# Activations or weights as the moving operand: the SwiGLU and output products of a four-layer encoder

## The chip, the core and the metric

The kernel runs on one core of a Trainium2 chip. The metric is device time in microseconds (us) of one execution, the median of several runs. TensorE (PE) multiplies: a load of weights (LDWEIGHTS, row PEld in the profile) puts a stationary operand of up to 128x128 into the array, and a MATMUL streams the columns of a moving operand past it and adds the result into a bank of PSUM, 128 partitions by 512 float32. VectorE (DVE), ScalarE (ACT) and GpSimd (POOL) work element by element, and SyncE (SP) and others start the transfers (DMA) from the main memory. Engines wait for each other by semaphores.

## The reference

Four layers, each with a token mixer and a SwiGLU, both behind an RMS norm and added to the residual. 256 tokens, 1024 features, 2816 hidden units, all float32.

```
for i in range(4):
    x = x + mixer[i % 3](rmsnorm(x, g_mix[i]))     # short convolution, attention, Hyena, short convolution
    h = rmsnorm(x, g_ffn[i])
    g, u = split(h @ w13[i])                       # 1024 -> 2 x 2816
    x = x + (silu(g) * u) @ w2[i]                  # 2816 -> 1024
```

Mixer A is `w_out((B * conv3(C * h)))`, mixer B an attention in a window of the 4 x 64 grid of tokens, mixer C a Hyena operator (two long convolutions as products with Fourier matrices; its filters depend on no input x and are made beside the SwiGLU stages of layers 0 and 1). Each mixer ends in an output projection of 1024 x 1024.

## The kernel before

*Layout.* The residual X lies by feature: 8 tiles of 128 features by 256 tokens (line 81). Every product of the trunk is made in three parts to keep float32's accuracy at the rate of float32r: with hi = the value rounded to float32r and lo the rest, hi*hi + hi*lo + lo*hi, which is `mm3` (lines 113 to 118). A weight piece of 128 x 1024 is loaded by SP (L104), rounded by ACT (L105) and its low part made by DVE or, for a share, by POOL (L108, recorded as L74). There are five buffers for loaded pieces and six for their parts, so pieces run some way ahead.

*Products.* In `mm3` the weight is stationary and the activation moves: 128 x 128 of the weight against 128 features x 256 tokens. Output tiles are by feature. Only mixer B's input product (`rows`, lines 493 to 502) has it the other way round, with 256 columns of the weight moving.

*Norm.* `Norm.add` (L134) multiplies a residual tile by the gain and splits it into the two parts xs (ACT L137, DVE L138) and squares it (ACT L155; DVE adds). The factor 1/rms belongs to a token, so it is applied to what comes out: `stats` (L158) turns the sum of squares by two PE transposes, `expand` (L173) turns 1/rms back and spreads it over all partitions as R.

*SwiGLU* (`ffn`, L259). w13: 11 pairs of hidden column tiles; for each pair four weight pieces (two of g, two of u), eight matmul triples each, into the banks pg and pu. A stage later `gated` multiplies both by R (tg, tu), takes Silu and the product (hh), and splits it into the two parts hid. w2: eight output tiles po of 22 triples; as each is done, `residual` (L184) adds it to X and prepares that tile of the next norm.

*Output projections* (`OutProj`, L202). The rows of w_out are taken as the mixer delivers its tiles: six of eight (AHEAD) go into all eight output tiles at once, four banks; for the last two, `finish` goes output tile by output tile, each followed by its residual and norm tile. The first products after a norm go through the k tiles in the order in which these come (`in_group`).

*Order.* The program is recorded in the order of the code, with stages of the pipelines delayed by slots of a weight piece each (`Pipeline`), and a scheduler then sets the order of each engine by what is ready. `fill(j)` lets the Hyena filters go on by a step at given places of the SwiGLU. Each engine works through its own list in that fixed order; a PSUM bank or a part buffer is taken again when its last reader is done.

In names of tiles, digits tell layers and numbers: xsf2 is the norm of layer 2's SwiGLU (xsf; f0 to f3), xsm3 that of layer 3's mixer (m0 to m3), hiw and low the parts of a SwiGLU weight, accco the output projection of mixer C.

Of the kernel before, what the change touches and what calls it, by code (L numbers as in the profile page):

```python
# [9 lines left out]
F32 = mybir.dt.float32  # L10
# [8 lines left out]
P = 128  # L19
# [10 lines left out]
# columns of the per-partition vector table  # L30
# [21 lines left out]
def encoder(ctx: ExitStack, tc: tile.TileContext, A: dict, out: bass.AP):  # L52
# [23 lines left out]
    def v2(a):  # L76
        """[P, 512] as two halves."""
        return a.rearrange("p (i t) -> p i t", i=2)

# [1 line left out]
    X = const.tile([P, KT, T], F32, name="X")  # L81
# [38 lines left out]
    def split(hl, src):  # L120
        """hl[:, 0] + hl[:, 1] = src, both float32r; the parts lie along axis 1."""
        ac.copy(out=hl[:, 0], in_=src)
        tt(hl[:, 1], src, hl[:, 0].bitcast(F32), ALU.subtract)

    class Norm:
        """The pre-norm of the next sub-layer: x times the gain as the operand of
        its products, and 1 / rms by token for what comes out of them."""

        def __init__(self, gcol, name):
            self.g, self.name, self.xs, self.late = gcol, name, {}, []  # L130
            self.ss = tp.tile([P, T], F32, tag="ss", name=f"ss{name}", bufs=2)
            self.R, self.some = None, False

        def add(self, m, square=True):  # L134
            xm, g = X[:, m, :], vec[:, self.g + m : self.g + m + 1]
            xs = xsp.tile([P, 2, T], F32R, tag="xs", name=f"xs{self.name}_{m}")
            ac.activation(xs[:, 0], xm, AF.Copy, scale=g)  # L137
            ve.scalar_tensor_tensor(  # L138
                out=xs[:, 1], in0=xm, scalar=g, in1=xs[:, 0].bitcast(F32),
# [3 lines left out]
            if square:  # L143
                self.square(m)
            else:
                self.late.append(m)

        def square(self, m):
            xm = X[:, m, :]
            if not self.some:  # L150
                self.some = True
                ac.activation(self.ss, xm, AF.Square)
            else:
                sq = t1(f"sq{self.name}_{m}")
                ac.activation(sq, xm, AF.Square)  # L155
                tt(self.ss, self.ss, sq, ALU.add)

        def stats(self):  # L158
            """1 / rms, the tokens on the partitions."""
            n = self.name  # L160
            for m in self.late:
                self.square(m)
            ps = self.ps = bank(f"psn{n}")
            ms = tp.tile([P, 2], F32, tag="ms", name=f"ms{n}", bufs=2)
            for i in range(2):
                pe.transpose(ps[:, i * P : (i + 1) * P], self.ss[:, i * P : (i + 1) * P], ident)
            ve.tensor_reduce(out=ms, in_=ps[:, :T].rearrange("p (i f) -> p i f", i=2), axis=AX.X, op=ALU.add)
            ve.tensor_scalar(out=ms, in0=ms, scalar1=1.0 / D, scalar2=EPS,
                             op0=ALU.mult, op1=ALU.add)
            rt = self.rt = tp.tile([P, 2], F32, tag="rt", name=f"rt{n}", bufs=2)  # L170
# [13 lines left out]
    def residual(m, ps, norm):  # L184
        tt(X[:, m, :], X[:, m, :], ps, ALU.add)
        if norm is not None:
            norm.add(m)
# [743 lines left out]
```

## Time and profile before

| what | us |
|---|---|
| three runs | 1257.48, 1259.48, 1259.76 |
| median | 1259.48 |
| span of the profiled execution | 1256.2 |
| mean granted TensorE clock of it | 0.990 of 2.4 GHz |
| matmuls and weight loads recorded | 10,034 each |
| PE busy in the span | 1219.3 (97%) |
| VectorE, ScalarE, GpSimd | 913.4, 634.6, 269.8 |
| moved by DMA | 228.90 MB, 182 GB/s in the mean |

The profile is of one execution; its span goes from its first instruction to its last, and what the device adds around it is in the runs' times alone (1.3 to 3.6 us here). A matmul is recorded with a modelled end, so that successive ones overlap: the distance from start to start tells the pace, not the duration. The granted clock is the share of 2.4 GHz that the chip gives TensorE; it is 1.00 in most stretches and 0.50 in a few.

### The profile page before, as it was taken

To read this page: it belongs to the slowest core of one execution; us is meant where nothing else is said; L and a number is where in the kernel's file an instruction comes from. 1 tells how busy PE (TensorE), PEld (TensorE's weight loads), DVE (VectorE), ACT (ScalarE), POOL (GpSimd) and SP (SyncE) were. 2 spreads that over 40 slices of the span, in tenths; PEclk is the share of its full clock that TensorE was granted. 3 is DMA by queue.
4 is the path that set the end of the run, shared out by engine and by line. 5 is a ranking of instruction groups with operands and counts; after the bars stand their busy time and mean duration, and the time that the engine had idled before them with its cause. 6 is when DMAs were issued, how large, how long until landed. Compare 5 with 4: busy or idle time off the path is not lost.

```text
span 1256.2 us, 24460 instructions
## 1 busy us (share of the span) xinstructions
PE 1219.3 (97%) x10034; PEld 1211.2 (96%) x10034; DVE 913.4 (73%) x1156; ACT 634.6 (51%) x931; POOL 269.8 (21%) x228
## 2 busy tenths in 40 slices
PE   7999999999999999999988979999999999999998
PEld 7999999999998999999988879999999999999998
DVE  7766877887776688878869997766655676766642
ACT  6545554555667554545544345444444455444431
POOL 0111122333454023213347773000000000000000
PEclk9999999999999999999998989999999999999999
DMA  9556556666666365666754324655566565655571
GB/s 307 184 175 229 185 173 193 201 191 222 209 178 194 118 218 186 192 187 191 232 179 135 121 98 155 199 184 185 173 185 197 176 188 163 199 185 185 170 203 46
DMA packets 68505, 228.90 MB, mean 182 GB/s; under 512 B 9831, under 2 KB 11241, under 8 KB 68265
## 3 DMA queue, kind: packets, MB, share of 16 engines
q1 hardware_dynamic: 61408, 211.68, 53.8%
q0 software_dynamic: 4656, 9.73, 2.6%
q10 hardware_dynamic: 2328, 5.93, 1.4%
q8 instruction: 78, 1.28, 0.4%
q14 instruction: 35, 0.28, 0.1%
HBM read 220.99 MB, written 6.29 MB: 181 GB/s over the span
## 4 chain that ended last, share of the span: by engine, by line
PE 84%; DVE 8%; issue 2%; ACT 2%; DMA 2%; POOL 2%; SPq 0%; ACTq 0%; DVEq 0%; POOLq 0%
PE pu L116 7%; PE pg L116 7%; PE pg L118 7%; PE pu L117 7%; PE pg L117 7%; PE pu L118 7%; PE po L116 7%; PE po L118 7%; PE po L117 7%; DVE a L74 1%; PE ai1a L117 1%; PE ai1a L116 1%; PE ai1a L118 1%; PE accao L116 1%; PE accao L117 1%
## 5 line engine op out<-in xcount | busy, mean ns | idle before, releaser
L105 ACT CAST hiw<-stw 128x1024 fp32r<-128x1024 f32 (+1 forms) x276 | 280.5, 1024 | 314.3 <-PE pg L117 85.3
L74 DVE TENSOR_TENSOR low<-stw,hiw 128x1024 fp32r<-128x1024 f32 (+1 forms) x254 | 306.2, 1212 | 155.1 <-ACT hiw L105 153.8
L116 PE MATMUL pu<-xsf,hiw 128*128 128x256 f32 x704 | 199.9, 284 | 0.0
L116 PE MATMUL pg<-xsf,hiw 128*128 128x256 f32 x704 | 199.3, 283 | 0.0
L118 PE MATMUL pg<-xsf,low 128*128 128x256 f32 x704 | 199.2, 283 | 0.0
L117 PE MATMUL pu<-xsf,hiw 128*128 128x256 f32 x704 | 199.2, 283 | 0.0
L117 PE MATMUL pg<-xsf,hiw 128*128 128x256 f32 x704 | 199.2, 283 | 0.0
L118 PE MATMUL pu<-xsf,low 128*128 128x256 f32 x704 | 199.2, 283 | 0.0
L116 PE MATMUL po<-hid,hiw 128*128 128x256 f32 x704 | 197.5, 281 | 0.0
L117 PE MATMUL po<-hid,hiw 128*128 128x256 f32 x704 | 197.5, 281 | 0.0
L118 PE MATMUL po<-hid,low 128*128 128x256 f32 x704 | 197.5, 281 | 0.0
L116 PEld LDWEIGHTS pg<-xsf,hiw 128*128 128x128 f32 x704 | 134.6, 191 | 0.3 <-issue 0.3
L116 PEld LDWEIGHTS pu<-xsf,hiw 128*128 128x128 f32 x704 | 134.5, 191 | 0.3 <-ACT hiw L105 0.3
L118 PEld LDWEIGHTS pg<-xsf,low 128*128 128x128 f32 x704 | 134.6, 191 | 0.0
L117 PEld LDWEIGHTS pg<-xsf,hiw 128*128 128x128 f32 x704 | 134.6, 191 | 0.0
L117 PEld LDWEIGHTS pu<-xsf,hiw 128*128 128x128 f32 x704 | 134.6, 191 | 0.0
L118 PEld LDWEIGHTS pu<-xsf,low 128*128 128x128 f32 x704 | 134.5, 191 | 0.0
L116 PEld LDWEIGHTS po<-hid,hiw 128*128 128x128 f32 x704 | 132.4, 188 | 0.0
L117 PEld LDWEIGHTS po<-hid,hiw 128*128 128x128 f32 x704 | 132.4, 188 | 0.0
L118 PEld LDWEIGHTS po<-hid,low 128*128 128x128 f32 x704 | 132.4, 188 | 0.0
L74 POOL TENSOR_TENSOR low<-stw,hiw 128x1024 fp32r<-128x1024 f32 (+1 forms) x22 | 53.6, 2434 | 158.8 <-ACT hiw L105 150.8
L105 ACT CAST hiai<-stai 128x1024 fp32r<-128x1024 f32 (+1 forms) x49 | 49.0, 1014 | 49.0 <-issue 13.3
(246 smaller groups left out, 2922.3 us busy)
## 6 DMA issues: line engine op xcount, KB each, us to landing
stw<-in_f_w SPq DMA_DIRECT2D x208, 512.0 KB, 3.6
stw<-in_f_w SPq DMA_DIRECT2D x64, 448.0 KB, 3.4
stai<-in_a_w_in SPq DMA_DIRECT2D x45, 512.0 KB, 3.7
stbi<-in_b_w_qkv SPq DMA_DIRECT2D x24, 512.0 KB, 4.3
stci<-in_c_w_in SPq DMA_DIRECT2D x24, 512.0 KB, 4.0
stao<-in_a_w_out SPq DMA_DIRECT2D x16, 512.0 KB, 4.3
hf<-ht POOLq DMA_DIRECT2D x16, 256.0 KB, 2.7
stbo<-in_b_w_out SPq DMA_DIRECT2D x8, 512.0 KB, 4.0
```

Of the source, the lines that this page charges most:

```text
L74: (eng or ve).tensor_tensor(out=out_, in0=a, in1=b, op=op)
L105: ac.copy(out=hi[:, c], in_=st[:, c])
L116: pe.matmul(ps, hi[:, ws], xh, start=first, stop=False, **kw)
L117: pe.matmul(ps, hi[:, ws], xl, start=False, stop=False, **kw)
L118: pe.matmul(ps, lo[:, ws], xh, start=False, stop=last, **kw)
```

## The change

The residual X now lies by token (two tiles of 128 tokens by 1024 features), and in SwiGLU and in the output projections the activation is the stationary operand, 128 x 128 of it, while 512 columns of the weight stream past.

- w13: a pair of hidden tiles has two banks, one for each half of the tokens, with 256 columns of g beside 256 of u. Silu and the product then work by token, where 1/rms is one value per partition: ACT's scale and DVE's scalar take the place of R. The gated tile hh is by token and must be by hidden unit to be stationary in w2: `turned` turns it by four PE transposes into a bank, from which it is split.
- w2 and the output projections: one class `OutProj` for both. All output is in four banks (two halves of the features by two of the tokens). The rows of the weight are taken as they come, up to the last four (w2, HELD) or three (AHEAD is 5); for those it goes bank by bank, and each bank is added to X when it is done.
- Norm: the next sub-layer still needs x by feature. `turn` turns a bank's worth of X (four transposes, one norm has four such turns), ACT and DVE make the xs tiles from PSUM, and ACT squares X by token with the sum as an extra output. The last of the four turns, `flush`, comes within the next sub-layer's first products, after half of their k tiles.
- The input comes once by feature, for the first norm, and once by token, 1 MB, in mixer A. The output leaves by token in four transfers of 256 KB.
- The weights w13 and w2 lie in main memory in the order in which they are now loaded.

The input products of mixers A, B and C are as before. Comments are left out of the code.

```diff
-AHEAD = 6  # rows of an output projection that are taken as they come
+TURN_LAG = 1
+AHEAD = 5
+HELD = 4
...
-    X = const.tile([P, KT, T], F32, name="X")
+    X = const.tile([P, 2, D], F32, name="X")
...
+    def matmul3(ps, xh, xl, hi, lo, first, last):
+        pe.matmul(ps, xh, hi, start=first, stop=False, skip_group_check=True)
+        pe.matmul(ps, xl, hi, start=False, stop=False, skip_group_check=True)
+        pe.matmul(ps, xh, lo, start=False, stop=last, skip_group_check=True)
...
+        def turn(self, c, h):
+            if h == 0:
+                self.banks[c] = [bank(f"pt{self.name}{c}{i}") for i in range(2)]
+            for i in range(4):
+                pe.transpose(self.banks[c][i % 2][:, i // 2 * T + h * P : i // 2 * T + (h + 1) * P],
+                             X[:, h, c * 512 + i * P : c * 512 + (i + 1) * P], ident)
+            if h:
+                for i in range(4):
+                    self.part(4 * c + i, self.banks[c][i % 2][:, i // 2 * T : (i // 2 + 1) * T])
+                for h in range(2):
+                    self.square(c, h)
...
+        def square(self, c, h):
+            sq = t2(f"sq{self.name}{c}{h}")
+            ac.activation(sq, X[:, h, c * 512 : (c + 1) * 512], AF.Square, accum_out=self.ss[:, h, c : c + 1])
...
-        for n, (k, xs) in enumerate(norm.xs.items()):
+        for k in range(KT):
+            if k == KT // 2:
+                norm.flush()
+            xs = norm.xs[k]
...
-        def mul(self, m, k, mid):
-            mm3(self.acc[m // 2][:, (m % 2) * T : (m % 2 + 1) * T], self.parts[k],
-                slice(m * P, (m + 1) * P), mid[:, 0], mid[:, 1],
-                k == 0 and m % 2 == 0, k == KT - 1, skip=True)
+        def mul(self, c, h, k, mid):
+            hi, lo = self.parts[k]
+            t, cs = slice(h * P, (h + 1) * P), slice(c * 512, (c + 1) * 512)
+            matmul3(self.acc[c, h], mid[:, 0, t], mid[:, 1, t], hi[:, cs], lo[:, cs], k == 0, k == self.n - 1)
...
+            for c, h in self.acc:
+                for k in range(self.ahead, self.n):
+                    self.mul(c, h, k, mids[k])
+                xm = X[:, h, c * 512 : (c + 1) * 512]
+                tt(xm, xm, self.acc[c, h], ALU.add)
+                if norm is None:
+                    sy.dma_start(out=out[h][:, c * 512 : (c + 1) * 512], in_=xm)
+                elif before:
+                    norm.turn(*before)
+                before = c, h
...
-                tg, tu = t2(f"tg{layer}_{j}"), t2(f"tu{layer}_{j}")
-                tt(v2(tg), v2(pg), norm.R2(), ALU.mult)
-                sg = t2(f"sg{layer}_{j}")
-                ac.activation(sg, tg, AF.Silu)
-                tt(v2(tu), v2(pu), norm.R2(), ALU.mult)
                 hh = t2(f"hh{layer}_{j}")
-                tt(hh, sg, tu, ALU.mult)
-                h = hp.tile([P, 2, 2, T], F32R, tag="hid", name=f"hid{layer}_{j}")
-                split(h.rearrange("p i s t -> p s i t"), v2(hh))
-                hid.append(h)
-                fill(j)
+                for h in range(2):
+                    r = norm.rt[:, h : h + 1]
+                    sg = t1(f"sg{layer}_{j}{h}")
+                    ac.activation(sg, ps[h][:, :T], AF.Silu, scale=r)
+                    ve.scalar_tensor_tensor(out=hh[:, h * T : (h + 1) * T], in0=ps[h][:, T:], scalar=r, in1=sg,
+                                            op0=ALU.mult, op1=ALU.mult)
+                line.add(line.now + TURN_LAG, turned, j, hh)
...
+            def turned(j, hh):
+                pt = bank(f"pth{layer}_{j}")
+                for i in range(2):
+                    for h in range(2):
+                        pe.transpose(pt[:, i * T + h * P : i * T + (h + 1) * P],
+                                     hh[:, h * T + i * P : h * T + (i + 1) * P], ident)
+                h = hp.tile([P, 2, 2, T], F32R, tag="hid", name=f"hid{layer}_{j}")
+                split(h.rearrange("p i s t -> p s i t"), v2(pt))
+                hid.extend([h[:, 0], h[:, 1]])
+                fill(j)
...
+            for k in range(FT - HELD):
+                if k == 16:
+                    share[0] = 0
+                op.step(k, hid[k] if k < len(hid) else None)
                 line.tick()
...
+                if k % 2 and k < 16:
+                    fill(NP_ + k // 2)
...
+                if ia == 0 and m == 3:
+                    sy.dma_start(out=X, in_=A["xt"])
```

How the instructions move is shown at two places. On PE, at the end of layer 2's SwiGLU, before: po2_7 is the last output tile, ai1a0 the first product of mixer A in layer 3, whose norm is xsm3.

```order
L116 MATMUL po2_7_11691<-hid2_10_11046,hiw2_2_7_15_11750 128x256
L117 MATMUL po2_7_11691<-hid2_10_11046,hiw2_2_7_15_11750 128x256
L118 MATMUL po2_7_11691<-hid2_10_11046,low2_2_7_15_11751 128x256
L116 MATMUL ai1a0_11792<-xsm3_0_11135,hiai10_0_11795 128x256
L117 MATMUL ai1a0_11792<-xsm3_0_11135,hiai10_0_11795 128x256
L118 MATMUL ai1a0_11792<-xsm3_0_11135,loai10_0_11796 128x256
```

And now, one bank before that end: accw2_2_01 and accw2_2_10 are the second and third of w2's banks, ptm300 and ptm301 the banks for the turned residual.

```order
L130 MATMUL accw2_2_01_8727<-hiw2_2_21_9088,hid2_10_8778 128x512
L131 MATMUL accw2_2_01_8727<-low2_2_21_9089,hid2_10_8778 128x512
L158 MATMUL ptm300_9119<-ident_77,X_75 128x128
L158 MATMUL ptm301_9120<-ident_77,X_75 128x128
L158 MATMUL ptm300_9119<-ident_77,X_75 128x128
L158 MATMUL ptm301_9120<-ident_77,X_75 128x128
L129 MATMUL accw2_2_10_8728<-hiw2_2_18_9070,hid2_9_8687 128x512
```

The turn of each bank stands behind the next bank's products; the products have 512 columns. The last turn on PE, here in the first pair of layer 2's w13 (pg2_00 and pg2_01 are the first pair's banks, pg2_10 and pg2_11 the second's, xsf2_4 is the first norm tile that needs this turn):

```order
L131 MATMUL pg2_01_7738<-low13_2_01_7759,xsf2_3_7708 128x512
L158 MATMUL ptf210_7725<-ident_77,X_75 128x128
L158 MATMUL ptf211_7726<-ident_77,X_75 128x128
L158 MATMUL ptf210_7725<-ident_77,X_75 128x128
L158 MATMUL ptf211_7726<-ident_77,X_75 128x128
L129 MATMUL pg2_10_7831<-hiw13_2_10_7834,xsf2_0_7699 128x512
L130 MATMUL pg2_10_7831<-hiw13_2_10_7834,xsf2_0_7699 128x512
L131 MATMUL pg2_10_7831<-low13_2_10_7835,xsf2_0_7699 128x512
L129 MATMUL pg2_11_7832<-hiw13_2_10_7834,xsf2_0_7699 128x512
L129 MATMUL pg2_00_7737<-hiw13_2_02_7776,xsf2_4_7785 128x512
L129 MATMUL pg2_01_7738<-hiw13_2_02_7776,xsf2_4_7785 128x512
```

Between the turn and the first use of its norm tile stand four products of the second pair (a fifth follows after the two of xsf2_4). On DVE, the gate of a pair in layer 2 (number 3), before:

```order
L74 TENSOR_TENSOR low13_2_30_10182<-stw13_2_30_10180,hiw13_2_30_10181 128x1024
L74 TENSOR_TENSOR tg2_3_10139<-pg2_3_9974,Rf2_9798 128x512
L74 TENSOR_TENSOR low13_2_31_10212<-stw13_2_31_10210,hiw13_2_31_10211 128x1024
L74 TENSOR_TENSOR low13_2_10_10244<-stw13_2_10_10242,hiw13_2_10_10243 128x1024
L74 TENSOR_TENSOR tu2_3_10140<-pu2_3_9975,Rf2_9798 128x512
L74 TENSOR_TENSOR hh2_3_10145<-sg2_3_10142,tu2_3_10140 128x512
L74 TENSOR_TENSOR low13_2_11_10285<-stw13_2_11_10283,hiw13_2_11_10284 128x1024
L74 TENSOR_TENSOR hid2_3_10147<-hh2_3_10145,hid2_3_10147 128x2x256
```

and now:

```order
L76 TENSOR_TENSOR low13_2_50_8196<-stw13_2_50_8194,hiw13_2_50_8195 128x1024
L321 SCALAR_TENSOR_TENSOR hh2_3_8123<-pg2_30_8014,rtf2_7854,sg2_30_8124 128x256
L76 TENSOR_TENSOR low13_2_51_8221<-stw13_2_51_8219,hiw13_2_51_8220 128x1024
L321 SCALAR_TENSOR_TENSOR hh2_3_8123<-pg2_31_8015,rtf2_7854,sg2_31_8127 128x256
L76 TENSOR_TENSOR low13_2_52_8247<-stw13_2_52_8245,hiw13_2_52_8246 128x1024
L76 TENSOR_TENSOR low13_2_53_8265<-stw13_2_53_8263,hiw13_2_53_8264 128x1024
L76 TENSOR_TENSOR hid2_3_8153<-pth2_3_8148,hid2_3_8153 128x2x256
```

Two half-size products take the place of three, and the split of hid reads the turned tile pth.

## Rows read from the trace of the kernel before

**Rows 1.** Page, busy us, share of the span and number of instructions

```profile
PE 1219.3 (97%) x10034; PEld 1211.2 (96%) x10034; DVE 913.4 (73%) x1156; ACT 634.6 (51%) x931; POOL 269.8 (21%) x228
```

**Rows 2.** Page, chain that ended last, shares by engine

```profile
PE 84%; DVE 8%; issue 2%; ACT 2%; DMA 2%; POOL 2%; SPq 0%; ACTq 0%; DVEq 0%; POOLq 0%
```

**Rows 3.** Windows by stage: stretch, length, busy us per engine, clock, DMA share

```profile
237.30:304.50 67.20, 67.20 (x574) 67.20 (x573) 58.34 (x77) 35.91 (x52) 18.23 (x17) 1.00 0.66 199
...
394.80:426.90 32.10, 30.26 (x255) 29.53 (x254) 21.95 (x38) 20.50 (x51) 6.34 (x7) 1.00 0.56 179
...
626.50:757.90 131.40, 112.65 (x806) 108.87 (x805) 114.11 (x107) 59.74 (x97) 90.12 (x59) 0.91 0.41 133
...
780.70:907.80 127.10, 127.10 (x1062) 127.10 (x1062) 85.58 (x102) 61.32 (x75) 0.71 (x1) 1.00 0.57 180
907.80:970.50 62.70, 62.70 (x531) 62.70 (x530) 37.31 (x47) 29.45 (x39) 0.00 (x0) 1.00 0.64 188
...
1040.10:1062.80 22.70, 22.70 (x194) 22.70 (x193) 14.02 (x22) 11.85 (x19) 0.64 (x1) 1.00 0.60 186
```

**Rows 4.** Timeline in w13: start us, us, engine, line, instruction, shapes

```profile
149.99 0.28 PE L116 MATMUL pu<-xsf,hiw 128*128 128x256 f32 x1
149.99 0.19 PEld L117 LDWEIGHTS pu<-xsf,hiw 128*128 128x128 f32 x1
150.11 0.28 PE L117 MATMUL pu<-xsf,hiw 128*128 128x256 f32 x1
```

**Rows 5.** Timeline of PE in mixer C

```profile
676.02 0.41 PE L116 MATMUL ci<-xsm,hici 128*128 128x256 f32 x1
676.24 0.41 PE L117 MATMUL ci<-xsm,hici 128*128 128x256 f32 x1
```

**Rows 6.** Windows, two short stretches (PE, PEld, DVE, ACT, POOL busy; clock)

```profile
343.00:345.00 2.00, 2.00 (x20) 2.00 (x19) 2.00 (x3) 2.00 (x3) 0.35 (x1) 1.00 0.93 197
...
676.00:679.20 3.20, 3.20 (x17) 3.20 (x16) 3.20 (x4) 0.50 (x2) 3.13 (x4) 0.50 0.51 164
```

**Rows 7.** Timeline of PE in mixer C, the product yi and what follows

```profile
665.15 1.89 PE L734 MATMUL yi<-a,dfti 128*128 128x256 f32 x8
666.88 0.39 PE L678 MATMUL ut<-ident,cx 128*128 128x128 f32 x2
```

**Rows 8.** Tile yi: weight loads, duration ns min/median/max

```profile
L734 PEld LDWEIGHTS yi<-a,dfti x32: 186/190/192, 665.0 to 702.3; 128*128 128x128 f32 x32
```

**Rows 9.** Timeline of PE in mixer B: two groups of transposes

```profile
343.26 0.60 PE L475 MATMUL ppt<-ident,pr 128*128 128x128 f32 x4
343.69 0.60 PE L441 MATMUL pqt<-ident,qn 128*128 128x128 f32 x4
344.05 0.36 PE L500 MATMUL bi<-hibi,xsm 128*128 128x256 f32 x1
344.25 0.28 PE L501 MATMUL bi<-hibi,xsm 128*128 128x256 f32 x1
```

**Rows 10.** Tile pqt: weight loads of transposes, duration ns min/median/max

```profile
L441 PEld LDWEIGHTS pqt<-ident,qn x32: 137/141/145, 329.0 to 403.5; 128*128 128x128 f32 x32
```

**Rows 11.** Groups by line and form, DVE and ACT: count | busy us, mean ns

```profile
L74 DVE TENSOR_TENSOR low<-stw,hiw 128x1024 fp32r<-128x1024 f32 x196 | 243.2, 1248 | 126.0 <-ACT hiw L105 124.8 <-POOL lr L74 1.2
...
L74 DVE TENSOR_TENSOR hh<-sg,tu 128x512 f32<-128x512 f32 x44 | 37.4, 851 | 2.1 <-DVE tu L74 0.5
...
L74 DVE TENSOR_TENSOR tg<-pg,Rf 128x512 f32<-128x512 f32 x44 | 30.2, 687 | 13.8 <-PE pg L118 13.7
...
L138 DVE SCALAR_TENSOR_TENSOR xsf<-X,vec,xsf 128x256 fp32r<-128x256 f32 x32 | 15.3, 479 | 0.1
...
L105 ACT CAST hiw<-stw 128x1024 fp32r<-128x1024 f32 x212 | 220.4, 1049 | 237.4 <-PE pg L117 80.8 <-issue 53.8 <-PE pu L117 52.6
...
L137 ACT ACTIVATE xsf<-X,vec 128x256 fp32r<-128x256 f32 x32 | 16.0, 500 | 6.3 <-DVE X L74 6.3
```

**Rows 12.** DMA issues: count, KB each, us to landing

```profile
out<-X SPq DMA_DIRECT2D x8, 128.0 KB, 1.9
```

More of the change, by code (lines that the diff above doesn't have):

```diff
@@ new lines, in expand, with R2, __init__, add @@
+        def expand(self):
+            n, ps = self.name, bank(f"psr{self.name}")
+            for i in range(2):
+                pe.transpose(ps[:, i * P : (i + 1) * P], self.rt[:, i : i + 1].broadcast_to([P, P]), ident)
+            self.R = tp.tile([P, T], F32, tag="R", name=f"R{n}", bufs=2)
+            ac.copy(out=self.R, in_=ps[:, :T])
+        def R2(self):
+            return self.R.unsqueeze(1).broadcast_to([P, 2, T])
+    class FirstNorm(Norm):
+        def __init__(self, gcol, name):
+            super().__init__(gcol, name)
+            self.todo, self.src = [], {}
+        def add(self, m, xm):
+            self.part(m, xm)
+            self.src[m] = xm
@@ L170, in stats @@
-            rt = self.rt = tp.tile([P, 2], F32, tag="rt", name=f"rt{n}", bufs=2)
-            gp.tensor_tensor(out=rt, in0=ms, in1=nhalf[:, :2], op=ALU.pow)
-        def expand(self):
-            n, ps, rt = self.name, self.ps, self.rt
-            for i in range(2):
-                pe.transpose(ps[:, T + i * P : T + (i + 1) * P], rt[:, i : i + 1].broadcast_to([P, P]), ident)
-            self.R = tp.tile([P, T], F32, tag="R", name=f"R{n}", bufs=2)
-            ac.copy(out=self.R, in_=ps[:, T:])
@@ L181, in R2 @@
-        def R2(self):
-            return self.R.unsqueeze(1).broadcast_to([P, 2, T])
[L184 to L187, printed above, removed]
+            ss = t1(f"ss{n}")
+            for m, xm in self.src.items():
+                if m == 0:
+                    ac.activation(ss, xm, AF.Square)
+                else:
+                    sq = t1(f"sq{n}_{m}")
+                    ac.activation(sq, xm, AF.Square)
+                    tt(ss, ss, sq, ALU.add)
@@ L194, in in_group, with __init__ @@
     def in_group(parts, norm):
-        for n, (k, xs) in enumerate(norm.xs.items()):
+        for k in range(KT):
+            if k == KT // 2:
+                norm.flush()
+            xs = norm.xs[k]
             for ps, w, first in parts:
                 mm3(ps, w, slice(k * P, (k + 1) * P), xs[:, 0], xs[:, 1],
-                    n == 0 and first, n == KT - 1, skip=True)
+                    k == 0 and first, k == KT - 1, skip=True)
     class OutProj:
-        def __init__(self, w, name, ahead):
-            self.w, self.name, self.ahead = w, name, ahead
+        def __init__(self, w, n, name, ahead):
+            self.w, self.n, self.name, self.ahead = w, n, name, ahead
@@ L295, in ffn @@
[L295 to L310 removed]
+                ps = [bank(f"pg{layer}_{j}{h}") for h in range(2)]
@@ new lines, in ffn @@
+                for p in range(KT // 2):
+                    hi, lo = wload(A["f_w13"][layer, j, p], D, f"w13_{layer}_{j}{p}")
+                    for k in (2 * p, 2 * p + 1):
+                        if j == 0 and k == KT // 2:
+                            norm.flush()
+                        c = slice(k % 2 * 512, (k % 2 + 1) * 512)
+                        for h in range(2):
+                            xh, xl = (norm.xs[k][:, i, h * P : (h + 1) * P] for i in range(2))
+                            matmul3(ps[h], xh, xl, hi[:, c], lo[:, c], k == 0, k == KT - 1)
+                    line.tick()
@@ L777, in mixer_c @@
             op.finish(mids, nxt)
-    norm = Norm(V_GM, "m0")
+    norm = FirstNorm(V_GM, "m0")
+    x0pool = ExitStack()
+    x0 = x0pool.enter_context(tc.tile_pool(name="x0", bufs=1)).tile([P, KT, T], F32, name="x0")
     def load_x(m0, m1):
-        (sy if m0 else ac).dma_start(out=X[:, m0:m1], in_=A["x"][:, m0:m1])
+        (sy if m0 else ac).dma_start(out=x0[:, m0:m1], in_=A["x"][:, m0:m1])
         for m in range(m0, m1):
-            norm.add(m, square=False)
+            norm.add(m, x0[:, m])
     load_x(0, 2)
@@ L899, in _layout @@
     wqkv = np.stack(cols).transpose(0, 1, 3, 2, 4, 5).reshape(12, 2, P, D)
+    w13 = i["f_w13"].reshape(4, KT // 2, 2, P, 2, NP_, T).transpose(0, 5, 1, 3, 2, 4, 6).reshape(4, NP_, KT // 2, P, D)
     twice = lambda a: np.concatenate([a, a], axis=-1)
```

123 lines of the change are left out of this document (47 added, 76 removed).

## The prediction

> **What bounds the kernel now.** I read the busy shares of the engines first. TensorE (PE) is busy 97% of the span of 1256.2 us, the VectorE (DVE), which makes the weights' low parts, 73% [rows 1]. The chain of waits says the same in another way: 84% of what ended last is PE itself, 8% DVE, 2% DMA [rows 2]. A busy PE need not be a PE at its best, so the next view is the table by stage [rows 3]. In the second half (layers 2 and 3) the SwiGLU stages have PE busy in every microsecond, with DVE at 67% and 60%: there nothing but PE's own pace counts. Two stages are different: mixer C (626 to 758 us), where DVE is busy 114 of 131 us and PE 113, and the end of mixer B (395 to 427 us). In the second product of SwiGLU in layer 0, DVE has 58 of 67 us, because the Hyena filters are made there.
>
> So the question is at what pace PE goes. Two successive starts in a w13 product are 0.12 us apart, and each start has its own weight load [rows 4]. At full clock (2.4 GHz) 256 columns take 106.7 ns, so 13 ns of each start are not streaming. What these 13 ns are decides the case. Three rows help. At a granted clock of 0.50 (the 1.2 GHz level) the same instructions start 213 ns apart, which is 256 columns at one per cycle with nothing on top [rows 5, 6]; so 512 columns at full clock cannot take less than 213. The product yi, with 256 columns of plain float32, has a stream twice as long: eight of them go from 665.15 to 666.88, 216 ns each, with 2 to 3 ns on top [rows 7], and its weight load is recorded with the same 190 ns as that of the w13 product [rows 4, 8]. And the PE transposes, whose weight load is recorded with 141 ns [rows 10], start 0.109 us apart although they too keep the array for 107 ns [rows 9]. Where the load is shorter than the stream, 2 to 3 ns are lost; where load and stream seem equally long, 13. I read this as a load that only just fails to hide behind 256 columns.
>
> **The change, part by part.**
>
> *Matmuls.* In SwiGLU a layer has 1056 matmuls of 256 columns in w13 and 528 in w2; an output projection has 192. Four of each make 7104. The undisturbed stages are 127.1, 62.7 and 22.7 us long [rows 3], four times each 850.0 us (the first holds the four transposes of the norm's statistics). Afterwards half as many, 3552, stream 512 columns each. The trace shows no 512-column matmul. Its bounds: 213.3 ns from below (rows 5, half the time for a column and twice the columns); 240 from above, twice the present 120; between them 226.7, if the 13 ns are paid at every change of weights. I take 216, the row of yi, which has the same length of stream and of load: 3552 x 0.216 = 767.2 us. Gain 82.8.
>
> *Transposes.* The hidden tiles are turned: 4 transposes per pair of column tiles, 11 pairs, 4 layers, 176. The residual is turned for seven norms, 16 each, 112. Together 288 at 109 ns, 31.4 us. Removed are six of the statistics of m1 to m3 (0.7; those of the four f norms are in the stages already). The 109 ns holds at both ends of a burst: eight transposes and the matmul after them take 0.99 us, from 343.26 to 344.25 [rows 9], 8 x 0.109 and that matmul's 0.12. The granted clock in that stretch is 1.00 [rows 6]. Against this change speaks the Trainium skill, "TensorE: Matmul & The Clock Gate", Part 4: about 275 ns for a transpose in a kernel, and transposes do not keep the clock up. By that figure they would cost 288 x 0.275 = 79 us and not 31; the clock, at least, holds in this trace.
>
> Sum on PE: 850.0 - 767.2 - 31.4 + 0.7 = 52.1 us saved; 1256.2 - 52.1 = 1204.1.
>
> *DVE and ACT at the gate.* Per pair DVE did three products of 128x512 (two of 0.69, one of 0.85) and a split; now two fused products of 128x256 (0.48, the shape of xsf) and the split, some 1.3 us less. ACT does two Silu of 256 columns for one of 512, and the norm's squares are summed on ACT where DVE added them. With four weight pieces of 1.25 us on DVE and 1.05 on ACT [rows 11] a pair costs DVE 4 x 1.25 + 2 x 0.48 + 0.85 = 6.8 us and ACT 4 x 1.05 + three of at most 0.6 = 6.0, while PE takes 48 x 0.216 + 0.44 = 10.8 (127.1 / 11 = 11.5 before). Both stay hidden; price nothing. The hidden tile's new path (gate, turn, split) is a slot longer; its reader is in w2, for the last pair 20 weight pieces later.
>
> *Where PE must wait anew.* (a) At each of seven junctions the last quarter of the residual is turned in the middle of the next sub-layer's first products, and its four norm tiles (ACT 0.50, DVE 0.48 each [rows 11]) come after that. The order puts four 512-column matmuls of the next pair behind those transposes, 0.9 us, and then two that need the norm tile from ACT alone. ACT's first tile is there after about 0.6, DVE's after 1.2, unless a weight piece of 1.25 stands ahead of it on DVE. From nothing to 2.2 us each; I take 0.5, for seven 3.5. (b) In the w2 product of layers 0 and 1 two steps of the filters were 132 matmuls apart, 15.7 us, and are now four pieces apart, 48 x 0.216 = 10.4 us; DVE has 58 of 67 us there. From nothing to 11.4 (both stages as long as before: 2 x (62.7 - 57.0)); I take 4. (c) At the end of mixer B PE fills the attention's waits with rows of the output product, six before, five now, each shorter. From nothing to 4.4 us (PE's idle 1.8 of that stage [rows 3], and 12 x 0.216 = 2.6 for the row that is missing); I take 1.5. (d) Mixer C starts with four norm tiles on its busy DVE, 4 x 0.48 = 1.9: from -1 to 3; I take 1. (e) At the very end the last addition is 128x512 (0.69, as tg) for 128x256, and the last store 256 KB for 128 KB, which took 1.9 us to land [rows 12]. 0.3 to 1.9; I take 1.1. Together 11.1. The 1 MB of x by token comes on SP's queue in mixer A, two weight pieces' worth of transfer ahead of weights that are loaded five pieces early: nothing.
>
> 1204.1 + 11.1 = 1215.2 us of span. The runs' median, 1259.5, lies 3.3 us above the profiled span; I keep that: **1218.5**.
>
> **The rivals.**
> *The 13 ns are paid at every change of weights.* Then 3552 x (226.7 - 216) = 38 us more, 1256.5. For it: in w2 the same shape goes at 62.7 us / 528 = 118.8 ns, in w13 at 120, so the loss depends on operands and not on length alone. Against it: neither transposes nor yi pay it, and they change weights as often.
> *The stream itself is slower than the array* (slower than before). If moving float32r data comes in at 256 columns per 120 ns, 512 take 240: 3552 x (240 - 216) = 85 us more, 1304. Its place is every SwiGLU and output product; it decides against the change from about 227.5 ns per matmul on (1259.5 - 1218.5 = 41 us over 3552). For it: the only float32r streams of the trace run at 0.12, and yi reads its moving data at half that rate. Against it: at half clock it is exactly a column a cycle, though a limit of supply would not show there.
> *Transposes cost their recorded duration*, because each is waited for. Four are recorded with 0.60 us and start 0.109 apart, so one lasts 0.60 - 3 x 0.109 = 0.273 [rows 9]; 288 x (0.273 - 0.109) = 47 us, 1265.5. Against it: two groups of four from different producers follow each other without a hole there. (The figure in Part 4 of that page of the Trainium skill is of this kind.)
> *DVE is the bound after all* at the junctions, with the filters, in B and in C: (a) to (d) at their upper ends, 15 + 11 + 4 + 3 = 33 instead of 10 us: 1242.
> That the change does not do what it says is excluded by its order of instructions, which has 3552 matmuls of 128x512.
>
> **How the numbers follow.** Likeliest, 216 ns and small waits: 0.70, own range 1203 (213.3 ns, -9.6, and half of the waits) to 1235. Paid handoff 0.11, slow stream 0.09, costly transposes 0.04, DVE 0.06. What a measurement can tell from no change is about 0.2%, 2.5 us. The paid handoff is faster half the time, else the same or slower alike; DVE and the likeliest are faster but for 0.02. That makes faster 0.80, same 0.05, slower 0.15. The range holds the likeliest with its bounds, DVE, and the paid handoff with 5 us on top, and leaves out the slow stream and the costly transposes: 1200 to 1262.
>
> **What would show it.** Right: successive w13 starts 216 ns apart, the SwiGLU stages of layers 2 and 3 about 119 and 57 us long, output projections near 21, transposes 0.109 apart in bursts of 0.44 at a granted clock of 1.00. Wrong: starts at 227 or 240; gaps on PE of 2 us and more behind the turns of the residual, ended by ACT or DVE; in layers 0 and 1 a PE that waits for pm or the low parts; mixer C longer than 134 us. The forecast stands or falls with the distance of the starts: a nanosecond there is 3.6 us.

## The result: 0.6% slower, where 3% faster was forecast

The changed kernel takes 1266.1 us (median of 4 runs, 1265.6 to 1268.2), the kernel before 1259.2 (1257.5 to 1259.8) beside it: a ratio of 1.006, 95% interval 1.0045 to 1.0074. The forecast was 1218.5, its range 1200 to 1262. The profiled execution's span is 1263.7 us, 7.5 more than that of before.

Read as before, the page puts TensorE (PE) at the top again. Busy times and counts, which answer to [rows 1]:

```profile
PE 1217.6 (96%) x6748; PEld 1055.2 (84%) x6748; DVE 841.5 (67%) x1023; ACT 636.2 (50%) x963; POOL 272.9 (22%) x228
```

A third of PE's instructions are gone and its busy time has hardly moved; VectorE (DVE) has 72 us less to do. The chain of waits still has 84% of PE, as in [rows 2]. So the time is where it was looked for, in the pace of the matmuls. The windows by stage, same columns as [rows 3]: w2 of layer 0, w13 and w2 of layer 2, the output projection of layer 3:

```profile
237.40:307.60 70.20, 70.20 (x340) 57.91 (x338) 54.16 (x63) 31.37 (x42) 20.92 (x22) 1.00 0.57 184
...
792.20:917.70 125.50, 125.50 (x576) 103.43 (x574) 73.58 (x84) 63.45 (x84) 1.61 (x1) 1.00 0.62 189
917.70:979.80 62.10, 62.10 (x280) 51.02 (x279) 28.89 (x29) 25.17 (x32) 0.00 (x0) 1.00 0.53 169
1049.90:1073.20 23.30, 23.30 (x111) 19.19 (x109) 12.67 (x18) 11.44 (x20) 0.64 (x1) 1.00 0.53 159
```

The two SwiGLU windows of layer 2 have no idle PE and a clock of 1.00, and yet last 125.5 and 62.1 us; forecast were 119 and 57. The timeline of PE says why. In w13 (start, us, instruction), what answers to [rows 4]:

```profile
860.57 0.39 PE L131 MATMUL pg<-low,xsf 128*128 128x512 f32 x1
860.80 0.39 PE L129 MATMUL pg<-hiw,xsf 128*128 128x512 f32 x1
861.02 0.39 PE L130 MATMUL pg<-hiw,xsf 128*128 128x512 f32 x1
861.25 0.39 PE L131 MATMUL pg<-low,xsf 128*128 128x512 f32 x1
```

and in w2:

```profile
940.59 0.39 PE L131 MATMUL accw<-low,hid 128*128 128x512 f32 x1
940.82 0.39 PE L129 MATMUL accw<-hiw,hid 128*128 128x512 f32 x1
941.05 0.39 PE L130 MATMUL accw<-hiw,hid 128*128 128x512 f32 x1
941.28 0.39 PE L131 MATMUL accw<-low,hid 128*128 128x512 f32 x1
```

Three matmuls take 0.68 us in w13 and 0.69 in w2: 227 and 230 ns each, not 216. Over the whole trace, without those behind a transpose or a wait, the mean distance is 227.7 ns in w13, 231.1 in w2, 229 in the output projections of mixers A and C and 233.9 in that of mixer B. Two 256-column matmuls took 240.0 in w13, 236.0 in w2, 237.4 in the projections of A and C and 234.2 in that of B. The transposes (here one burst of four between matmuls) are as forecast:

```profile
866.01 0.40 PE L131 MATMUL pg<-low,xsf 128*128 128x512 f32 x1
866.25 0.60 PE L329 MATMUL pth<-ident,hh 128*128 128x128 f32 x4
866.60 0.48 PE L129 MATMUL pg<-hiw,xsf 128*128 128x512 f32 x1
866.92 0.40 PE L130 MATMUL pg<-hiw,xsf 128*128 128x512 f32 x1
```

From 866.01 to 866.92 there are two matmuls and four transposes, 0.91 us; less 2 x 0.227 that leaves 0.114 for a transpose, 0.109 between starts inside the burst.

Stage lengths in us, from the first product of one stage to the first of the next, layers 0 to 3:

| stage | before | after |
|---|---|---|
| mixer, in-products | 73.7, 90.3, 131.5, 69.6 | 72.1, 93.9, 131.8, 70.1 |
| output projection | 22.8, 32.2, 22.8, 22.8 | 23.2, 31.8, 23.2, 23.2 |
| w13 | 134.6, 133.3, 127.1, 127.1 | 135.2, 130.6, 125.5, 125.6 |
| w2 | 67.2, 66.3, 62.7, 66.2 | 70.2, 73.3, 62.2, 64.9 |

SwiGLU won 2.1 and 2.8 us in layers 2 and 3 and lost 3.6 and 4.3 in layers 0 and 1, which also make the filters; mixer B lost 3.6 in its first products. The longest of PE's waits in these three places (line, releaser, us, times, longest):

```profile
PE pth L329 <- DVE hh L321: 2.0, 1, 2.0
PE bi L551 <- DVE lobi L76: 2.0, 1, 2.0
PE fl L682 <- ACT lr L679: 1.8, 1, 1.8
PE bi L550 <- DVE xsm L147: 1.7, 1, 1.7
```

### The profile page after: what moved, and what is told of

Same layout as the page of the kernel before. It is cut to its first block, busy times and chain, and to the rows that moved or that the text cites. A ratio compares the mean times of both kernels' runs of the same rounds, so it can differ in the third digit from the quotient of the medians.

```text
span 1263.7 us, 17703 instructions
## 1 busy us (share of the span) xinstructions
PE 1217.6 (96%) x6748; PEld 1055.2 (84%) x6748; DVE 841.5 (67%) x1023; ACT 636.2 (50%) x963; POOL 272.9 (22%) x228
## 4 chain that ended last, share of the span: by engine, by line
PE 84%; DVE 9%; issue 2%; POOL 2%; ACT 2%; DMA 2%; ACTq 0%; SPq 0%; DVEq 0%; POOLq 0%
PE pg L129 13%; PE pg L131 13%; PE pg L130 13%; PE accw L129 6%; PE accw L131 6%; PE accw L130 6%; PE pth L329 2%; PE ai1a L118 1%; PE ai0a L119 1%; PE ai1a L119 1%; PE ai1a L120 1%; DMA bm<-in_rpb 1%; PE ai0a L120 1%; PE ai0a L118 1%; PE accao L131 1%
## 5 line engine op out<-in xcount | busy, mean ns | idle before, releaser
L76 DVE TENSOR_TENSOR low<-stw,hiw 128x1024 fp32r<-128x1024 f32 x246 | 304.8, 1243 | 225.9 <-ACT hiw L107 224.3
L107 ACT CAST hiw<-stw 128x1024 fp32r<-128x1024 f32 x268 | 280.7, 1052 | 298.6 <-PE pg L130 142.2
L129 PE MATMUL pg<-hiw,xsf 128*128 128x512 f32 x704 | 278.5, 397 | 0.5 <-ACT xsf L146 0.5
L131 PE MATMUL pg<-low,xsf 128*128 128x512 f32 x704 | 275.0, 391 | 0.0
L130 PE MATMUL pg<-hiw,xsf 128*128 128x512 f32 x704 | 274.3, 390 | 0.0
L131 PEld LDWEIGHTS pg<-low,xsf 128*128 128x128 f32 x704 | 132.4, 188 | 28.5
L129 PEld LDWEIGHTS pg<-hiw,xsf 128*128 128x128 f32 x704 | 132.4, 188 | 28.3 <-ACT xsf L146 1.9
L130 PEld LDWEIGHTS pg<-hiw,xsf 128*128 128x128 f32 x704 | 132.7, 188 | 26.6 <-DVE xsf L147 0.2
L129 PE MATMUL accw<-hiw,hid 128*128 128x512 f32 x352 | 139.7, 397 | 0.0
L131 PE MATMUL accw<-low,hid 128*128 128x512 f32 x352 | 138.5, 393 | 0.0
L130 PE MATMUL accw<-hiw,hid 128*128 128x512 f32 x352 | 138.0, 392 | 0.0
L131 PEld LDWEIGHTS accw<-low,hid 128*128 128x128 f32 x352 | 66.0, 188 | 15.9
L130 PEld LDWEIGHTS accw<-hiw,hid 128*128 128x128 f32 x352 | 66.2, 188 | 14.6
L129 PEld LDWEIGHTS accw<-hiw,hid 128*128 128x128 f32 x352 | 66.3, 188 | 14.0
L76 DVE TENSOR_TENSOR loai<-stai,hiai 128x1024 fp32r<-128x1024 f32 (+1 forms) x49 | 56.9, 1178 | 15.7 <-ACT hiai L107 15.4
```

Source lines behind the costliest of these rows:

```text
L76: (eng or ve).tensor_tensor(out=out_, in0=a, in1=b, op=op)
L107: ac.copy(out=hi[:, c], in_=st[:, c])
L129: pe.matmul(ps, xh, hi, start=first, stop=False, skip_group_check=True)
L130: pe.matmul(ps, xl, hi, start=False, stop=False, skip_group_check=True)
L131: pe.matmul(ps, xh, lo, start=False, stop=last, skip_group_check=True)
```

## The experiments

Distances between starts below are worked out from the first starts of two successive blocks, divided by the count. The theories are (A) a fixed price of each weight change, (B) load and stream disturb each other, (C) traffic of other engines. The programs of blocks ran once each.

**The pace by itself.**

> The kernel leaves the encoder out: TensorE alone runs blocks of 64 matmuls, all other engines idle. Three theories of what each 512-column float32r matmul costs beside its 213.3 ns of stream. (A) A fixed price of a weight change, about 13 ns whatever the shapes: 226.7 ns for 512 columns, 173.3 for 384, 120 for 256; the same 226.7 with a stationary operand of 64 or of 32 columns. (B) The load of the weights disturbs the stream while it lasts: 13 ns with 128 stationary columns, 6 to 7 with 64, 3 to 4 with 32, so 227, 220 and 217. (C) Traffic of the other engines and DMAs: 214 to 216 here, where all of them are still. The prediction's own reading (a load that only just fails to hide) wants 214 to 216 as well, and 120 again with 256 columns. bf16 blocks beside them show whether the price belongs to float32r: under (A) bf16 pays it too. Plain float32 with 256 columns: 216 as in the row of yi; with 512 columns 428 to 430.

The timeline of PE, one row a block (r is float32r, b bf16, f plain float32, the number the columns):

```profile
19.66 14.67 PE L44 MATMUL rn512x<-wr,xr 128*128 128x512 f32 x64
34.16 11.28 PE L44 MATMUL rn384x<-wr,xr 128*128 128x384 f32 x64
45.28 7.83 PE L44 MATMUL rn256x<-wr,xr 128*128 128x256 f32 x64
52.95 7.26 PE L44 MATMUL rn128x<-wr,xr 128*128 128x128 f32 x64
...
133.19 13.99 PE L44 MATMUL bn512x<-wb,xb 128*128 128x512 bf16 x62
147.01 7.15 PE L44 MATMUL bn256x<-wb,xb 128*128 128x256 bf16 x64
...
157.57 55.15 PE L44 MATMUL fn512x<-w,x 128*128 128x512 f32 x128
212.56 27.79 PE L44 MATMUL fn256x<-w,x 128*128 128x256 f32 x128
240.19 14.45 PE L44 MATMUL fn128x<-w,x 128*128 128x128 f32 x128
```

float32r: 226.6 ns for 512 columns, 173.8 for 384, 119.8 for 256: 13.3, 13.8 and 13.1 above the stream, at every length. bf16 takes 215.9 (by the 64 matmuls of the block, of which 62 were recorded) and plain float32 429.6 and 215.9 (a record of plain float32 lasts two cycles a column; 64 matmuls left 128 records): 2 to 3 above it. So the 13 ns go with the operand type, do not shrink when the stream is twice as long, and need no other engine. The row of yi [rows 7] was of a kind that does not pay them. (A) is not the whole of it either: with 64 stationary columns instead of 128, 256 moving ones go at 113.6, but 512 at 230.

**Traffic.** Blocks of 512 columns beside each engine's work.

> The kernel leaves the encoder out: blocks of 64 float32r matmuls of 512 columns, first with every other engine still, then beside a stream of DVE subtractions, of ACT copies, of POOL subtractions, of DMA loads, and of all of these at once. (A) and (B), a price of the weight change or of the load: every block within 1 ns of the quiet ones, about 227. (C), traffic: quiet blocks 214 to 216, and 225 to 235 beside one of the streams or beside all.

Windows (PE, PEld, DVE, ACT, POOL busy, clock, DMA share, GB/s) of a still block and of two beside everything:

```profile
17.00:31.00 14.00, 14.00 (x63) 11.59 (x62) 0.00 (x0) 0.00 (x0) 0.00 (x0) 1.00 0.00 1
...
165.00:190.00 25.00, 25.00 (x128) 21.38 (x127) 24.62 (x12) 10.34 (x10) 16.36 (x6) 1.00 0.57 240
```

and the first two of these blocks in the timeline:

```profile
19.21 14.67 PE L47 MATMUL quietax<-wr,xr 128*128 128x512 f32 x64
...
171.53 14.67 PE L47 MATMUL withalyx<-wr,xr 128*128 128x512 f32 x64
```

Every block of 64 lasts 14.67 us, beside DVE, ACT, POOL or DMA alone as well: 226.7 ns whatever the others do. (C) falls, for operands placed as in these blocks.

**w13 alone, and the rest alone.** The first is the kernel before with the new `gated`, `turned` and w13 loop only; the second the changed kernel with the old w13 loop only.

> Of the change only the first SwiGLU product: activations stationary, 512 weight columns, hidden rows turned by PE transposes; second product, output projections and residual by feature as before. If the matmul's price is what the profile after shows (230 ns where two of before took 240.6), each layer gains 528 x 10.6 ns = 5.6 us and pays 44 x 0.09 to 0.11 us = 4 to 4.8 us for the turns, so 0.8 to 1.6 us a layer, 3 to 6 us in all: 1253 to 1256 us, faster than before. If instead what the profile after lost in layers 0 and 1 (the filters' waits) comes from the first product, this version is no faster than before: 1259 or more.

1252.8 (1252.1 to 1253.8), ratio 0.995 (0.9938 to 0.9967): this half is faster than both kernels by a little, 124.7 us where w13 of layer 2 took 127.1.

> The other parts of the change without the first SwiGLU product: second product and output projections with activations stationary, residual by token, each norm turned by PE transposes; first product by feature as before, so no hidden rows are turned. By the stages of the profile after (out +0.4 each, w2 -0.5 and -1.3 in layers 2 and 3, w2 +3.0 and +7.0 in layers 0 and 1, mixer B +3.6) this part alone is slower than before: 1264 to 1271 us. If the loss belongs to the first product or to the turns of the hidden rows, it comes out at or below 1259.

1270.6 (1270.1 to 1273.3), ratio 1.010 (1.0078 to 1.0123). The loss is in this half: -6 and +12 us stand beside the whole change's +7.

**Addresses.** Two runs of TensorE alone.

> The kernel leaves the encoder out: TensorE alone, blocks of 24 equal float32r matmuls. The first look showed 213.3 + 13.4 ns for 512 columns at one pair of addresses, whatever the other engines did, 225 to 240 where the operands began elsewhere, and with 256 columns 113 instead of 120 when the stationary operand had 64 columns instead of 128. (A) A fixed price of the weight change: the same 226.7 at every address and every number of stationary columns, n/2.4 + 13.4 for every n. (B) Load and stream disturb each other while both read: the price changes with the address of either operand, in steps that repeat, and falls with the number of stationary columns (about 10 ns at 96, 7 at 64). If (B) holds there may be addresses at which the price is under 5 ns, that is 218 or less; if none of the 36 addresses goes under 223, no placement of tiles can bring the 216 that was predicted.

The price changes with the address of either operand, and within 2 ns it is the same for places 64 words apart. What counts is the distance of the two: the moving operand 16 words further gives 228.8 ns, the stationary one 48 words further 229.6. For lengths that are no multiple of 64 it changes as well (480 columns 216.7 ns, 500 223.4). None of the 36 addresses was under 226.7, so none of the places tried brings 216. The prediction of (B) that the price falls with the stationary columns did not hold at 512 (230 to 234 from 96 down to 16), at 256 roughly (118 at 112, 113 at 16).

> The kernel leaves the encoder out: TensorE alone; blocks of 44 float32r matmuls with 128 stationary columns; the moving operand begins 0, 2, 4 ... 62 words (32 places, 256 columns) or 0, 4 ... 60 words (16 places, 512 columns) further, modulo 64 words, than the stationary one. (B), in the form that the look at shapes left: what counts is the distance of the two operands' addresses modulo 64 words. With 512 columns 226.7 at distance 0, about 229 at 16, 230 to 234 elsewhere, nowhere under 225. With 256 columns 120 at 0 and something between 113 and 122 elsewhere, since the second SwiGLU product of the kernel before, with its operands 32 words apart, went at 117 where the first, at 0, went at 120. (A): 120 and 226.7 at every place.

Some of the blocks (a: 256 columns, b: 512; the number is the distance in words; 44 matmuls each):

```profile
21.24 5.43 PE L43 MATMUL a0x<-wr,xr 128*128 128x256 f32 x44
26.51 5.44 PE L43 MATMUL a2x<-wr,xr 128*128 128x256 f32 x44
...
126.34 5.32 PE L43 MATMUL a40x<-wr,xr 128*128 128x256 f32 x44
131.51 5.43 PE L43 MATMUL a42x<-wr,xr 128*128 128x256 f32 x44
...
147.30 5.17 PE L43 MATMUL a48x<-wr,xr 128*128 128x256 f32 x44
152.31 5.45 PE L43 MATMUL a50x<-wr,xr 128*128 128x256 f32 x44
...
209.32 10.43 PE L43 MATMUL b8x<-wr,xr 128*128 128x512 f32 x44
219.59 10.42 PE L43 MATMUL b12x<-wr,xr 128*128 128x512 f32 x44
229.85 10.24 PE L43 MATMUL b16x<-wr,xr 128*128 128x512 f32 x44
239.93 10.33 PE L43 MATMUL b20x<-wr,xr 128*128 128x512 f32 x44
```

With 512 columns 226.8 to 234.5, best at 60 and 0; with 256 columns 113.6 at 28 and 113.9 at 48 words, 117 to 121 nearly everywhere else (129.5 at 26). Held against the places that the tiles have in the two programs as they are built (distance of the moving operand from the stationary one, words modulo 64; ns, the kernels' as means by stage), the blocks give the pace of each product within 1 ns:

| product | distance | block | in the kernel |
|---|---|---|---|
| before: w13 | 0 | 119.8 | 120.0 |
| before: w2, layers 2 and 3 | 32 | 118.6 | 118.7 |
| before: w2, layers 0 and 1 | 40 | 117.5 | 117.3 |
| after: w13 | 0 | 227.7 | 227.4 to 227.9 |
| after: w2, layers 2 and 3; projections of A and C | 16 | 229.1 | 228.9 to 229.1 |
| after: w2, layers 0 and 1 | 8 | 233.4 | 233.3, 233.4 |
| after: projection of B | 40 | 234.3 | 233.9 |

The 117 ns that the expectation gives for 32 words is the pace of layers 0 and 1, at 40 words. That the pace goes with the distance is measured; what in the chip makes it so is not. Nor is the distance all, as the next two kernels show.

**The changed kernel, its tiles moved.**

```
+    tp.tile([P, 16], F32, tag="pad", name="padtp", bufs=1)
...
+        cp.tile([P, 56], F32, name="padf")      # filters
...
+            cp.tile([P, 32], F32, name="padb")  # mixer B
```

> The changed kernel with the tiles of the hidden rows and of the mixers' results moved by padding, so that they begin 0 words (modulo 64) from the weights instead of 48 or 56. Nothing else is changed. (B): their 512-column matmuls fall from a mean of 230 to 231 ns to 227, that is 4 ns x (1056 in the second SwiGLU product + 384 in the output projections) = 5 to 6 us less than the changed kernel: 1260 to 1261. (A): no change, 1266.

1261.7 (1260.9 to 1263.3), ratio 1.0025 (1.0014 to 1.0036), 4.4 us below the changed kernel, where 5 to 6 were expected. (The 48 and 56 of the expectation count from the weight to the other operand, 16 and 8 in the table; in mixer B it was 24, which is 40.) w2 in layer 2 now:

```profile
938.58 0.39 PE L133 MATMUL accw<-low,hid 128*128 128x512 f32 x1
938.80 0.39 PE L131 MATMUL accw<-hiw,hid 128*128 128x512 f32 x1
939.03 0.39 PE L132 MATMUL accw<-hiw,hid 128*128 128x512 f32 x1
939.25 0.39 PE L133 MATMUL accw<-low,hid 128*128 128x512 f32 x1
```

0.67 us for three, a mean of 227.0 in w2 where it was 231.1, and 227.7 in the projections of A and C. The projection of B, at distance 0 as well, goes at 231.0 (233.9 before): its matmuls come in bursts of seven to thirteen, and behind a break the first ones take 224 to 240 ns before they come down to 227. The distance counts in the kernel too.

**The kernel before, its tiles moved.** No instruction of the work is changed.

```
+    xsp.tile([P, 48], F32, tag="pad", name="padx", bufs=1)
+    wst.tile([P, 16], F32, tag="pad", name="padw", bufs=1)
+    tp.tile([P, 16], F32, tag="pad", name="padt", bufs=1)
...
+        cp.tile([P, 56], F32, name="padf")      # filters
...
+            cp.tile([P, 32], F32, name="padb")  # mixer B
```

> The kernel before, every weight stationary and 256 columns streamed as it was; only padding is added, so that the normed input, the hidden rows and the mixers' results begin 48 words (modulo 64) from the weights, where the blocks by themselves went at 113.9 ns instead of 119.8. (B): the products of the normed input (1056 a layer in SwiGLU, 576 in each of the mixers A and C) gain some 6 ns each, 32.9 us; the second SwiGLU product (117.4 before) 3.5 ns x 2112 = 7.4; the output projections (118.7) 4.8 ns x 768 = 3.7; mixer B, whose stationary and moving operands are the other way round (distance 16, 117.9), 2 ns x 576 = 1.2. Sum 45, so 1214; with some of it given back as waits for VectorE and weights in layers 0 to 2, 1210 to 1225. Its first SwiGLU product would then go at 2 x 114 = 228 ns for the work of one 512-column matmul, as fast as the changed kernel without any turn. (A): padding changes nothing, 1257 to 1261.

1222.2 (1220.8 to 1225.2), ratio 0.972 (0.9703 to 0.9735): the fastest of all, without a single turn. Layer 2's windows, to be held against [rows 3]:

```profile
768.90:889.00 120.10, 120.10 (x1062) 120.10 (x1061) 85.52 (x102) 61.42 (x75) 0.71 (x1) 1.00 0.61 190
889.00:948.90 59.90, 59.90 (x531) 59.90 (x531) 37.28 (x47) 29.50 (x39) 0.00 (x0) 1.00 0.65 196
```

120.1 and 59.9 us, the same instructions that took 127.1 and 62.7. SwiGLU's products go at 113.3 to 114.0 in layers 2 and 3, twice which is 227 to 228. It missed the 1214 expected: in layers 0 and 1 they go at 115.6 to 116.3 in the mean, w13 of layer 0 gained only 4 of 7 us, mixer C nothing (131.2; DVE is busy 118 of it), mixer A of layer 3 two of 3.5. The trace shows what the means hide: at this distance of 48 words there are two steady paces. In w13 of layer 0, first and thirteenth of thirteen successive matmuls at two places:

```profile
194.72 0.28 PE L122 MATMUL pu<-xsf,hiw 128*128 128x256 f32 x1
...
196.13 0.28 PE L122 MATMUL pg<-xsf,hiw 128*128 128x256 f32 x1
...
219.73 0.28 PE L122 MATMUL pg<-xsf,hiw 128*128 128x256 f32 x1
...
221.09 0.28 PE L122 MATMUL pg<-xsf,hiw 128*128 128x256 f32 x1
```

Twelve distances are 1.41 us at the first place and 1.36 at the second. From 187.5 to 209.9 us the pace is 117.8 ns throughout, then eight of the filters' products come in between, and from 211.1 to 229.9 it is 113.3 after the first few. So it goes through the whole trace: a run of products without a break keeps one of the two after its first few matmuls. Some 3100 of the 8700 products at this distance have the slower one, 14 us in all; in w13 and w2 of layers 2 and 3 it is only the first 165 in layer 3. What decides at a break which of the two follows, no run shows.

> The kernel before with padding of the same kind as in the kernel moved by 48 words, but to a distance of 24 words, where the blocks by themselves went at 120.0. (B), what counts is the distance: normed-input products as before (120), second SwiGLU product 117.4 to 120, +2.6 ns x 2112 = 5.5 us, output projections 118.7 to 120, +1, so 1263 to 1267, slower than before. If padding as such brought the gain (another layout of the tiles, whatever the distance), it is near 1222.

The same padding with 24, 40 and 56 words in place of 48, 16 and 16 for the first three: 1263.6 (1260.2 to 1264.5), ratio 1.003 (1.0015 to 1.0046). w13 at 120.0, w2 at 120.0 where it was 118.0. It is the distance, not the padding as such.

**The terms beside the pace.**

> The changed kernel with all eighteen pieces of the filters' work put into the first SwiGLU product (pieces 0 to 9 and 0 to 7 instead of every second slot over both products). Two theories of what layers 0 and 1 lose (their SwiGLU stages come out 3.6 and 4.3 us longer than before, those of layers 2 and 3 2.1 and 2.8 shorter). (F) The filters' pieces stand too close in the second product, where a slot is now two weight rows: then the second product falls from 70.2 and 73.3 to 62 to 64 us, the first grows by no more than the products that move into it (4 to 5 us a layer), and the whole is 6 to 12 us shorter, 1254 to 1260. (G) VectorE and ScalarE have no more room in the first product than in the second: what the second wins, the first loses in waits for hidden rows, and the whole is within 3 us of 1266, or longer.

`FILTER_SLOTS = (range(0, 10), range(0, 8))`. 1268.0 (1267.1 to 1269.0), ratio 1.007 (1.0052 to 1.0091). w13 and w2 of layer 0:

```profile
102.80:246.10 143.30, 140.15 (x667) 115.94 (x666) 122.66 (x154) 76.01 (x110) 47.45 (x42) 0.99 0.64 200
246.10:309.40 63.30, 63.30 (x281) 50.97 (x280) 26.58 (x27) 25.29 (x32) 4.94 (x3) 1.00 0.55 172
```

w2 falls to 63.3 in both layers, as (F) said, but w13 grows by 8.1 and 9.3, so that the time is the one that (G) gave. The waits that (G) names are not what grew most: PE is idle for 3.1 us of w13 in each of the two layers, where it was 2.5 and 0 in the changed kernel, and 2.7 us of that in all are waits for hidden rows. The larger part is the filters' own products: they took 7.0 and 8.0 us of w2 in the changed kernel, not the 4 to 5 that (F) reckoned with. Moving the filters' work moves its time.

> The changed kernel with every transpose of a hidden row issued twice, 176 more of them. At the 0.109 us between starts, all of it on the path of TensorE: +19.2 us, 1285. If TensorE waits for the hidden rows anyway where they stand, less than +10. If a transpose costs its recorded duration of 0.27 us, +48, 1314.

`for i in (0, 1, 0, 1):` around the transposes. 1281.8 (1277.6 to 1282.6), 15.7 above the changed kernel, 89 ns for each of 176. The windows of w13 and w2 in layer 2 are 129.6 and 62.6 us for 125.5 and 62.1, 44 transposes for 4.6 us or 105 ns each; in w13 of layer 0, where PE waits for hidden rows, nothing is added (135.3 for 135.2). They are on PE's path, at well under half of their recorded duration.

## Why the prediction was wrong

*PE as the bound, and the count of its work*: right. 3552 matmuls of 512 columns stand where 7104 were, and the undisturbed windows have no idle PE.

*The price of a 512-column matmul, 216 ns from the row of yi*: this is the step that failed. I read the 13 ns of each start as "a load that only just fails to hide behind 256 columns", which a stream twice as long would hide. It does not. The blocks show 13 ns with 256, 384 and 512 columns alike, and 2 to 3 for plain float32 and bf16: [rows 7] and [rows 9] were rows of another operand type. The miss, from the means of the trace: 2112 x 11.7 ns in w13, 1056 x 15.1 in w2, 192 x 13.1, 96 x 13 and 96 x 17.9 in the projections: 24.7 + 15.9 + 5.5 = 46.1 us. 1218.5 + 46.1 = 1264.6; 1266.1 was measured. The Trainium skill, "TensorE: Matmul & The Clock Gate", Part 2, "Back-to-back issue gap", gives 518 cycles as the gap of a 512-column matmul, by estimate 215.8 ns at 2.4 GHz. The bf16 block agrees (215.9), the float32r block does not (226.6), and the measurement decides.

*The rival of a paid handoff* had nearly the size, 226.7 ns. Its reason for doubt ("neither transposes nor yi pay it") was the same mistake for yi and, by their operand type, for the transposes. What took the time past it is the distance of the operands: the hidden rows and the mixers' results lay 8, 16 or 40 words off (modulo 64), worth 1.4 to 7 ns by the table, and the moved tiles gave 4.4 us of it back. The hint was in the prediction, w2 at 118.8 and w13 at 120 [rows 3], and was not followed. *The rival of a slow stream* falls by the same blocks: 128 columns more cost 52.8 to 54.0 ns, about a column a cycle (53.3). The turning point named there, about 227.5 ns, was right: the mean over all came to 229, and the kernel is slower.

*Transposes at 0.109 us, 31 us together*: right in size by the trace and by doubling them; the recorded 0.273 us is not what one costs here. Nor is the 275 ns of the Trainium skill, "TensorE: Matmul & The Clock Gate", Part 4, "PE-mode transpose": doubling 176 of them cost 89 ns each.

*DVE and ACT at the gate at nothing*: right in layers 2 and 3. In layer 0 one burst waited 2.0 us for hh.

*The waits, 11.1 together*: nearly right as a sum, since matmuls (-82.8 + 46.1) and transposes (+30.7) leave 7.5 + 6.0 = 13.5 of the span for them. But this is luck, for the sum was wrongly divided. (b), waits for the filters in w2 of layers 0 and 1, was 4 with an upper end of 11.4. Layers 0 and 1 together lost nearly 13 us against layers 2 and 3, of which the distances explain 3.8 by the table (2 x 264 x 4.4 ns, and 2 x 528 x 1.4 ns in the kernel before, where w2 was the faster in those layers). Of the other 9, 5.1 are idle PE: 2.5 in w13 of layer 0 and 2.6 in w2 of layer 1, while w2 of layer 0 has none. The rest is not taken apart here, but a wait costs more than its length, as w2 of layer 1 shows:

```profile
582.10 0.42 PE L119 MATMUL fh<-pm,dfth 128*128 128x256 f32 x1
582.31 0.41 PE L120 MATMUL fh<-pm,dfth 128*128 128x256 f32 x1
```

PE has stood still there for 1.8 us (the wait for lr above) and for 0.7 more, and afterwards the filters' products start 0.213 us apart for 2.4 us, the pace of the 1.2 GHz level (the window 581.0 to 584.5 has 0.57 granted). Mixer B's start, the junction of (a), had 2.0 and 1.7 us of waits for DVE, and that stage lost 3.6; the other junctions and (c) to (e) cost little: the projection of B came out 0.4 us shorter, mixer C 0.3 longer, w2 of layer 3 with the end is 1.3 us shorter than before.

## What to carry to other kernels

Take the price of an instruction only from a row of its own operand type: a fixed part and a part that shrinks look alike at one length, and one block at a second length, on a still chip, tells them apart. Before a loop is turned round for a few ns per matmul, move its operands: here padding of some hundred bytes a partition brought 3%, and the rebuilt loop with its transposes nothing as a whole and 0.5% at best (w13 alone). An engine without idle time can still lose 6% inside its instructions.

## What the hardware showed unexpectedly

A float32r matmul with 128 stationary columns costs its stream plus 13 ns (13.1 to 13.8 for 256, 384 and 512 columns) when both operands begin at the same place modulo 64 words. At other distances it is 7 to 23 ns for 256 columns and 13 to 21 for 512, steady or in short repeating patterns, with every other engine still. One distance can have two paces (113.3 and 117.8 ns at 48 words and 256 columns), and a block by itself shows only one of them. The same weights loaded again and again pay it as well (227.1). Short streams meet a floor: 128, 192 and 224 columns all take 111 ns. The Trainium skill, "TensorE: Matmul & The Clock Gate", Part 2, "Step-by-step: what each phase is for", has two independent read ports, so that loading the next weights takes nothing from the running matmul. That a change of nothing but the distance between the two operands' addresses changes the time is hard to square with it for float32r; whether load and stream meet at the memory or elsewhere no run here settles, nor why 64 stationary columns help at 256 moving ones and not at 512.
